# Strassen products for three index pairs of the convolution side in a one-core hybrid encoder layer

## The chip, the core and the metric

The kernel runs on 1 core of one Trainium2 chip (trn2). The time is that of one execution on the device, in microseconds (us); the median of several runs is given. One further execution was recorded by the hardware profiler, and every row below comes from it. Its span is the time from its first to its last instruction.

## The reference

One layer on 512 tokens behind 16 meta tokens (528 in all), model width 2048, float32:

```
hn = rmsnorm(h_res) * norm_in_g
P = hn @ w_in                     # 2048 x 8320
Pr, Pc = P[..., :RW_COLS], P[..., RW_COLS:]
...                               # RWKV-7 on Pr: token shift, decay, delta-rule state per head -> y_a
Bg, Cg, hc, g_c = four parts of Pc, 1024 columns each
y_b = Bg * causal_depthwise_conv(Cg * hc, conv_w, width 3) * silu(g_c)
h_res = h_res + concat([y_a, y_b]) @ w_out
out = rmsnorm(h_res)[:, 16:]
```

The recurrence runs over time: in chunks of 64 tokens it needs, for each pair of heads, decays, Gram matrices and an inverse, which are prepared ahead of it.

## The kernel before

Channels lie on partitions and time on the free axis. A float32 product is made of three float32r ones: the operand is cast to a high part, the rest is the low part, and high x high, high x low and low x high accumulate in one PSUM bank (`steps`, L314). The input x lives in SBUF split in this way (`xh`, `xl`, 16 slabs of 128 channels by 528 columns, scaled by the norm's gain).

The weights are 65 tiles of 128 output columns: r, k, v, g for eight pairs of heads, one low-rank tile, and B, C, h, gc for eight groups of the convolution side. A tile comes in two halves of 128 x 1024 (512 KB each). `prefetch` loads a half into one of three `raw` buffers through SP's DMA queue; `split_w` splits each of its two quarters: ScalarE (ACT) casts the high part (L124), VectorE (DVE) or GpSimd (POOL) subtracts for the low part (L125). There are six buffers each for high and low parts, so splits run at most three halves ahead of TensorE (PE). A tile is 96 matmuls of 256 to 264 columns, or 48 of 512 columns for B and gc. The order of tiles is the list `plan`; `stream` is the list of their halves (`halves` after the change).

PE's order is written out by hand. `mains` is a generator that yields after every matmul of a tile, and the preparation of the heads (`prepare`, `invert`) calls `fill(ns)` to run so much of it while other engines work; `until` runs it up to a given tile. `FW` holds these amounts. `later(ns, fn)` issues stores and loads after so much PE time. DVE, ACT, POOL and SP are ordered by a scheduler, and each then works in that fixed order: an instruction that waits holds up all behind it on its engine.

The stages in order: start (low rank, k0, r0, B0); preparation in four pairs of heads, with tiles as filler; recurrence over nine chunks (`recur`), with convolution tiles as filler; mixing; output projection, which already uses Strassen-Winograd products and sums of weights made by accumulating transfers (`add_by_transfer`, L1178: a DMA issued by POOL that adds to what lies at its destination). Before the change, the convolution tiles of indices 0 to 2 stand in the preparation, those of 3 to 7 in the recurrence and behind it.

The use of a tile is `use`: for the convolution side, C and h are scaled by the norm's factor and multiplied, the width-3 convolution is taken, then multiplied by B and by the gate of gc; the result goes to DRAM (`mixd`) until mixing.

Of the kernel before, what the change touches and what calls it, by code (L numbers as in the profile page):

```python
# [26 lines left out]
LP = NCH * CH  # L27
NPAIR = 8
ALPHA = -0.3032653298563167
RMS_EPS = 1e-6  # L30
# [46 lines left out]
def hymba_kernel(ctx: ExitStack, tc: tile.TileContext, xt, xtok, front, w_in, w_out, pv, lup, cst, msk, gf, out):  # L77
# [15 lines left out]
    gated = [dp.tile([P, SEQ], F32, tag=f"gated{j}", name=f"gated{j}", bufs=1) for j in range(NPAIR)]  # L93
    yd = dp.tile([2 * NPAIR * CH, SEQ], F32, tag="yd", name="yd", bufs=1)
    mixd = {j: dp.tile([P, SEQ], F32, tag=f"mixd{j}", name=f"mixd{j}", bufs=1) for j in range(NPAIR, KT)}

# [6 lines left out]

    stream = []
    plan = [("lora", 0), ("k", 0), ("r", 0), ("B", 0), ("v", 0), ("k", 1), ("r", 1), ("v", 1), ("g", 0), ("g", 1)]
    for j in range(0, NPAIR, 2):
        if j:
            plan += [(what, i) for i in (j, j + 1) for what in ("k", "r", "v")] + [("g", j), ("g", j + 1)]
        plan += [(what, j // 2) for what in ("C", "h", "B", "gc") if j or what != "B"]
    plan += [(what, i) for i in range(4, NPAIR) for what in ("C", "h", "B", "gc")]  # L110
    tile_of = {"r": 0, "k": 8, "v": 16, "g": 24, "lora": 32, "B": 33, "C": 41, "h": 49, "gc": 57}
    for what, i in plan:
        m = tile_of[what] + i
        stream += [w_in[m, :, 0:1024], w_in[m, :, 1024:2048]]
    stream[0:8] = [stream[j] for j in (0, 2, 4, 6, 1, 3, 5, 7)]
    N_IN = len(stream)
    stream += [w_out[0, g] for g in range(3)]
    quarters, chain, low = {}, {}, {}
    state = {"next": 0}

    def split_w(q, rq, eng):
# [4 lines left out]
        quarters[q] = (hi, lo)  # L126

    def prefetch(upto):
        while state["next"] < min(upto, len(stream) if chain else N_IN):
            j = state["next"]  # L130
            raw = chain[j - N_IN] if j >= N_IN else wp.tile([P, 1024], F32, tag="raw", name=f"wr{j}", bufs=3)
            state["dma"] = nc.sync.dma_start(raw, stream[j]).ins
            with tc.high_priority(offset=WEIGHTS):
                for q in range(2):
                    split_w(2 * j + q, raw[:, q * 512 : (q + 1) * 512], nc.gpsimd if q and 10 < j < N_IN else nc.vector)
            state["next"] = j + 1

    keep = ctx.enter_context(tc.tile_pool(name="keep", bufs=1, side="right"))
# [6 lines left out]
    rs = xp.tile([P, L], F32, name="rs")  # L145
    la = xp.tile([P, 2, L], F32R, name="la")
    ones = xp.tile([P, P + 2], F32R, name="ones")
    omm = xp.tile([P, 33], F32, name="omm")
    hv = xp.tile([P, 6, 8], F32, name="hv")
    hl = cp.tile([P, 2, 8], F32, name="hl")  # L150
    smask = xp.tile([P, NCH, CH], F32, name="smask")
    pm = ph1.enter_context(tc.tile_pool(name="pm", bufs=4, space=PSUM))
# [4 lines left out]

    tp = ph1.enter_context(tc.tile_pool(name="tp", bufs=1))

    def tr(name, dt=F32):  # L160
        return cq.tile([P, LP], dt, tag="tr", name=name, bufs=5)

    def tm(name):
        return tp.tile([P, LP], F32, tag="tm", name=name, bufs=3)


    warm = tp.tile([P, 1], F32, name="warm")
    nc.gpsimd.memset(warm, 0.0)
    cold = tp.tile([P, 512], F32, tag="tm", name="cold", bufs=3)
    nc.vector.memset(cold, 0.0)  # L170
# [34 lines left out]
    def load_w(n, tag):  # L205
        t = view(tag, 512)
        nc.sync.dma_start(t, stream[n][:, 512:1024])
        return t
# [112 lines left out]

    def main(j, ranges, name):
        prefetch(2 * j + 4)
        ps = banks(ranges, name, pm, "main")
        for k4 in range(4):
            if k4 == 1:
                prefetch(2 * j + 5)
            yield from steps(ps, ranges, k4, 4 * j + k4)
        return ps

    def scaled(ranges, ps, dst, base):
# [3 lines left out]
    def shift_full(ps, m, name, dst):  # L335
        pr = tp.tile([P, L + 1], F32, tag="pr", name=f"pr_{name}", bufs=2)
        nc.gpsimd.memset(pr[:, 0:1], 0.0)
        scaled(FULL, ps, pr, -1)
        sh = tm(f"sh_{name}")[:, 0:L]
        nc.scalar.activation(sh, pr[:, 0:L], AF.Copy, scale=col(V_MU, m))  # L340
        for (a, b), d in dst:
            nc.vector.scalar_tensor_tensor(
                out=d, in0=pr[:, a + 1 : b + 1], scalar=omm[:, m : m + 1], in1=sh[:, a:b], op0=ALU.mult, op1=ALU.add
            )

    def shift_real(ps, m, name, dst):
        pr = tp.tile([P, L + 1], F32, tag="pr", name=f"pr_{name}", bufs=2)
# [9 lines left out]

    def gate(g, name):
        th = tm(f"th_{name}")[:, 0:SEQ]
        nc.scalar.activation(th, g, AF.Tanh, scale=0.5)  # L360
        nc.vector.scalar_tensor_tensor(out=g, in0=th, scalar=1.0, in1=g, op0=ALU.add, op1=ALU.mult)
# [17 lines left out]
    def use(what, i, ps):  # L379
# [7 lines left out]
        elif what in ("r", "g"):  # L387
            t = cq.tile([P, SEQ], F32, tag=f"r{i % 2}" if what == "r" else "g", name=f"{what}{i}")
            shift_real(ps, tile_of[what] + i, f"{what}{i}", t)
# [8 lines left out]
        elif what == "h":  # L398
# [5 lines left out]
            nc.gpsimd.tensor_tensor(out=u[:, 0:n], in0=u[:, 0:n], in1=hh[:, 0:n], op=ALU.mult)  # L404
            cv = tp.tile([P, SEQ], F32, tag="cw", name=f"cv{i}")
            nc.scalar.activation(cv, u[:, 0:SEQ], AF.Copy, scale=col(V_CW, i))
# [5 lines left out]
            if i == 0:  # L412
                nc.gpsimd.tensor_tensor(out=cv, in0=cv, in1=got["B", 0], op=ALU.mult)
        elif what == "B":
            b = tm(f"b{i}")[:, 0:SEQ] if i else tp.tile([P, SEQ], F32, name="b0")
            with behind_of("split"):
                scaled(REAL, ps, b, META)
            got[what, i] = b
            if i:
# [15 lines left out]
    def token_scale_sums():  # L435
        pss = pi.tile([P, 8], F32, tag="misc", name="pss")
        for j, (a, b) in enumerate(((0, 128), (128, 256), (256, 384), (384, 512), (512, L))):
            nc.tensor.matmul(pss[0 : b - a, j : j + 1], accd[:, a:b], cs[:, C_ON : C_ON + 1], start=True, stop=True)
        var = tp.tile([P, 3, 8], F32, tag="nv", name="var0")
        nc.gpsimd.memset(var[:, 0], 1.0)  # L440
# [19 lines left out]
    def mains():  # L460
# [34 lines left out]
        use("B", 0, pd)  # L495
        for j in range(4, len(plan)):
            what, i = plan[j]
            rg = FULL if what in ("k", "v") else REAL if what in ("B", "gc") else TAIL
            ps = yield from main(j, rg, f"{what}{i}")
            if what == "B" and i < 4:  # L500
                state["split"] = low[4 * j + 4]
            use(what, i, ps)
# [36 lines left out]
    def until(*key):  # L539
        while key not in ready:  # L540
            step()
# [498 lines left out]
    for i in range(0, NPAIR, 2):  # L1040
        invert([prepare(i), prepare(i + 1)])
    until("g", NPAIR - 1)
    run_pending(float("inf"))
    ph2.close()
    with tc.tile_pool(name="ch", bufs=1, side="right", reuse_waits="tile") as ch:
        recur(ch)


# [69 lines left out]
    for _ in flow:  # L1118
        pass
    prefetch(len(stream))  # L1120
    ph1.close()
# [49 lines left out]
    def request(half, k, col, g):  # L1171
        t = wp.tile([P, 1024], F32, tag="raw", name=f"wo{half}{k}{col}{g}", bufs=3)
        state["dma"] = nc.sync.dma_start(t, rows_of(half, k, col, g)).ins
        straight[half, k, col, g] = t
# [321 lines left out]
```

## Time and profile before

| | |
|---|---|
| median of 3 runs | 1024.05 us (1023.93 to 1024.28) |
| span of the profiled execution | 1023.6 us (its own time is not listed apart; the span stands 0.45 under the median) |
| mean granted TensorE clock | 0.996 |
| PE busy | 1006.6 us, 9723 matmuls |
| DVE, ACT, POOL busy | 686.1, 393.8, 273.8 us |
| DMA | 174.82 MB, mean 171 GB/s |

A row of a profile names the line, engine, operation and tiles (output<-inputs). Busy time counts any time in which the engine had an instruction in flight; for PE, whose matmuls overlap, the duration in a row is longer than the distance from one matmul to the next. "Idle before <- X" names what ended an idle time. DMA share is the mean busy share of the 16 DMA engines.

### The profile page before, as it was taken

To read this page: it belongs to the slowest core of one execution; us is meant where nothing else is said; L and a number is where in the kernel's file an instruction comes from. 1 tells how busy PE (TensorE), PEld (TensorE's weight loads), DVE (VectorE), ACT (ScalarE), POOL (GpSimd) and SP (SyncE) were. 2 spreads that over 40 slices of the span, in tenths; PEclk is the share of its full clock that TensorE was granted. 3 is DMA by queue.
4 is the path that set the end of the run, shared out by engine and by line. 5 is a ranking of instruction groups with operands and counts; after the bars stand their busy time and mean duration, and the time that the engine had idled before them with its cause. 6 is when DMAs were issued, how large, how long until landed. Compare 5 with 4: busy or idle time off the path is not lost.

```text
span 1023.6 us, 23708 instructions
## 1 busy us (share of the span) xinstructions
PE 1006.6 (98%) x9723; PEld 919.0 (90%) x9723; DVE 686.1 (67%) x1239; ACT 393.8 (38%) x729; POOL 273.8 (27%) x292
## 2 busy tenths in 40 slices
PE   9999999999999999999999999999999999999996
PEld 8899998999988999998999998889889897787885
DVE  7677954587765569654669653244555697998787
ACT  7553423344313434322434322222222335445453
POOL 0122323233332323232322232123332332015001
PEclk9999999999999999999999999999999999999999
DMA  9526476546764364864263845867673688695754
GB/s 333 152 63 148 122 190 182 150 123 143 167 172 134 96 170 99 217 167 117 83 166 98 220 139 168 309 212 235 195 232 93 183 276 192 172 319 135 172 125 165
DMA packets 185036, 174.82 MB, mean 171 GB/s; under 512 B 121568, under 2 KB 142816, under 8 KB 184416
## 3 DMA queue, kind: packets, MB, share of 16 engines
q1 hardware_dynamic: 182336, 164.40, 55.8%
q0 software_dynamic: 2304, 8.39, 4.7%
q8 instruction: 76, 1.25, 0.5%
q10 hardware_dynamic: 288, 0.52, 0.1%
q14 instruction: 32, 0.26, 0.1%
HBM read 136.92 MB, written 36.35 MB: 169 GB/s over the span
## 4 chain that ended last, share of the span: by engine, by line
PE 68%; DVE 8%; DMA 4%; issue 2%; SPq 1%; ACT 1%; POOL 0%; DVEq 0%; ACTq 0%; POOLq 0%
PE ps_gc L314 8%; PE ps_h L314 8%; PE ps_B L314 7%; PE ps_k L314 7%; PE ps_v L314 7%; PE ps_C L314 7%; PE ps_g L314 7%; PE ps_r L314 7%; DVE ol L1193 3%; DMA wo<-in_w_out_dram 2%; PE M L1220 2%; PE g L659 1%; PE zs L984 1%; PE Q L1220 1%; DVE xb L1201 1%
## 5 line engine op out<-in xcount | busy, mean ns | idle before, releaser
L125 POOL TENSOR_TENSOR wl<-wr,wh 128x512 fp32r<-128x512 f32 x119 | 169.2, 1423 | 370.8 <-ACT wh L124 356.4
L124 ACT CAST wh<-wr 128x512 fp32r<-128x512 f32 x252 | 152.7, 618 | 294.8 <-PE ps_C L314 51.9
L125 DVE TENSOR_TENSOR wl<-wr,wh 128x512 fp32r<-128x512 f32 x133 | 100.9, 765 | 109.0 <-ACT wh L124 108.6
L314 PE MATMUL ps_k<-xh,wl 128*128 128x264 f32 x256 | 73.1, 286 | 1.1 <-DVE wl L125 1.1
L314 PE MATMUL ps_v<-xh,wh 128*128 128x264 f32 x256 | 73.0, 285 | 0.0
L314 PE MATMUL ps_h<-xh,wh 128*128 128x258 f32 (+1 forms) x256 | 72.8, 284 | 0.0
L314 PE MATMUL ps_k<-xh,wh 128*128 128x264 f32 x256 | 72.8, 284 | 0.0
L314 PE MATMUL ps_v<-xl,wh 128*128 128x264 f32 x256 | 72.7, 284 | 0.0
L314 PE MATMUL ps_v<-xh,wl 128*128 128x264 f32 x256 | 72.7, 284 | 0.0
L314 PE MATMUL ps_k<-xl,wh 128*128 128x264 f32 x256 | 72.6, 284 | 0.0
L314 PE MATMUL ps_C<-xh,wh 128*128 128x258 f32 (+1 forms) x256 | 72.6, 284 | 0.0
L314 PE MATMUL ps_h<-xh,wl 128*128 128x258 f32 (+1 forms) x256 | 72.3, 282 | 0.2 <-issue 0.2
L314 PE MATMUL ps_r<-xh,wh 128*128 128x258 f32 (+1 forms) x256 | 72.4, 283 | 0.0
L314 PE MATMUL ps_g<-xl,wh 128*128 128x258 f32 (+1 forms) x256 | 72.3, 282 | 0.0
L314 PE MATMUL ps_r<-xl,wh 128*128 128x258 f32 (+1 forms) x256 | 72.2, 282 | 0.0
L314 PE MATMUL ps_g<-xh,wl 128*128 128x258 f32 (+1 forms) x256 | 72.0, 281 | 0.0
L314 PE MATMUL ps_C<-xl,wh 128*128 128x258 f32 (+1 forms) x256 | 72.0, 281 | 0.0
L314 PE MATMUL ps_g<-xh,wh 128*128 128x258 f32 (+1 forms) x256 | 72.0, 281 | 0.0
L314 PE MATMUL ps_h<-xl,wh 128*128 128x258 f32 (+1 forms) x256 | 71.9, 281 | 0.0
L314 PE MATMUL ps_r<-xh,wl 128*128 128x258 f32 (+1 forms) x256 | 71.9, 281 | 0.0
L314 PE MATMUL ps_C<-xh,wl 128*128 128x258 f32 (+1 forms) x256 | 71.9, 281 | 0.0
L314 PE MATMUL ps_B<-xh,wl 128*128 128x512 f32 x128 | 51.3, 401 | 0.0
(353 smaller groups left out, 3006.2 us busy)
## 6 DMA issues: line engine op xcount, KB each, us to landing
wr<-in_w_in_dram SPq DMA_DIRECT2D x126, 512.0 KB
ct<-opd SPq DMA_DIRECT2D x64, 288.0 KB
wo<-in_w_out_dram SPq DMA_DIRECT2D x24, 512.0 KB
x<-in_w_out_dram POOLq DMA_DIRECT2D x16, 512.0 KB, 6.2
opd<-ar SPq DMA_DIRECT2D x8, 576.0 KB
opd<-gt SPq DMA_DIRECT2D x16, 288.0 KB
opd<-bt SPq DMA_DIRECT2D x64, 64.0 KB
x<-in_w_out_dram SPq DMA_DIRECT2D x8, 512.0 KB
```

The costliest lines, as they stand in the source:

```text
L124: nc.scalar.copy(hi, rq)
L125: low[q] = eng.tensor_tensor(out=lo, in0=rq, in1=hi.bitcast(F32), op=ALU.subtract).ins
L314: nc.tensor.matmul(ps[r], ww[:, w], xx[:, kt, a:b], start=(kt == 0 and n == 0), stop=(kt == KT - 1 and n == 2))
L659: nc.tensor.matmul(z[h][:, c - c0], bk[hs, c, h : h + 2, :].rearrange("p a s -> p (a s)"), ar[hs, c].rearrange("p a s -> p (a s)"), start= ...
L984: nc.tensor.matmul(d[hs, j], w, x[hs], start=(a == 0), stop=(a == b - 1))
L1193: nc.vector.tensor_tensor(out=lo, in0=rq, in1=hi.bitcast(F32), op=ALU.subtract)
L1201: nc.vector.tensor_tensor(out=h, in0=h, in1=ps, op=op)
L1220: nc.tensor.matmul(bank[s], left(prod, jj, m, s), w, start=(jj == 0 and n == 0), stop=(jj == 7 and n == 2))
```

## The change

For indices 1, 2 and 3 of the convolution side the pairs (C, h) and (B, gc) are computed by Strassen's seven products. The 2 x 2 blocks are: two halves of the 2048 input channels, two tiles of output columns, two halves of the time (columns from 14 and from 270). A product is 24 matmuls of 258 (C, h) or 256 (B, gc) columns, with K = 1024; there are 3 x 2 x 7 = 42. The name M5(2,1) means product M5 for index 2, pair (B, gc); the list SPREAD writes it 521.

- Sums of weights: M1, M2, M3 use a plain half. M5 and M7 load one half into a raw buffer, then POOL issues a transfer that adds another. M6 does so with two further halves, in a tile of its own (`Y`); M4 adds a fourth to what M6 used.
- Forms of x: the four quarters of x are scaled by the gain and stored to DRAM (`scaled_rows`); forms F6, F5, S3, F3 are loaded and added by transfers (`form`) and split into `fh`, `fl`, which hold one form at a time.
- Sums of products: M1, M2, M6, M4 are combined on ACT and DVE and stored to DRAM (`partd`); M5, M7, M3 are copied out of PSUM and added in DRAM by POOL's transfers (`take`).
- In the recurrence, `finish_couple` (Z1 to Z3) loads the results, and does what `use` did.
- The order: all 42 products stand in the preparation, among k, r, v, g; index 0's C, h, gc move to its end; g6 and g7 too. `solve` and `solve_first` in FW grow by 6000 ns. The three raw buffers get names of their own; several tiles move between pools; B0's result waits in DRAM.

The core of the diff:

```diff
+HW = 258
...
-    evac=34, start=1062, lora=2200, gram=8000, gram_b=13500, gram2=5500, misc=2000, v=2000, vt=1000, solve=24500, solve_first=30000,
+    evac=34, start=1062, lora=2200, gram=8000, gram_b=13500, gram2=5500, misc=2000, v=2000, vt=1000, solve=30500, solve_first=36000,
...
+SPREAD = (
+    "v0 X11 k1 X00 r1 X01 v1 F6 g0 g1 g2 g3 110 k2 210 610 r2 v2 410 111 k3 211 "
+    "611 r3 v3 X10 411 120 220 620 k4 r4 420 121 221 621 k5 v4 421 130 230 630 r5 v5 "
+    "430 131 231 631 k6 r6 431 F5 k7 v6 510 511 520 521 530 531 S3 r7 v7 710 711 720 "
+    "721 730 731 F3 g4 g5 310 311 320 321 330 331 g6 g7 C0 h0 gc0 C4 h4 Z1 B4 gc4 "
+    "C5 Z2 h5 B5 gc5 C6 Z3 h6 B6 gc6 C7 h7 B7 gc7"
+)
...
+        if item[0] == "M6":
+            jobs.append((max(free_at[-2], f - 14, form_of["F6",] + 2), f, "sum", item))
...
+        elif item[0] in ("M5", "M7"):
+            jobs.append((f - 6, f, "sum", item))
...
+    def start(job):
...
+        if prod == "M6":
+            t = fp.tile([P, 4 * HW], F32, tag="Y", name=f"y{i}{s}", bufs=2)[:, 0:1024]
+            parts_ = [(0, 0), (1, 0), (1, 1)]
+        else:
+            t = take_slot(f"x{prod}{i}{s}")
+            parts_ = [(1, 0), (0, 0) if prod == "M5" else (1, 1)]
+        state["dma"] = nc.sync.dma_start(t, half_of(i, s, *parts_[0])).ins
+        for p in parts_[1:]:
+            nc.gpsimd.dma_start(t, half_of(i, s, *p), accum_op=ALU.add)
...
+    def follow(item, t):
+        if item[0] == "M6":
+            nc.gpsimd.dma_start(t, half_of(item[1], item[2], 0, 1), accum_op=ALU.add)
...
+    def form(name):
+        first, *others = FORMS[name]
+        for c in range(2):
...
+            nc.sync.dma_start(t, quarters_d[first][:, ks])
+            for x in others:
+                nc.gpsimd.dma_start(t, quarters_d[x][:, ks], accum_op=ALU.add)
+            nc.scalar.copy(fh[:, ks], t)
+            nc.vector.tensor_tensor(out=fl[:, ks], in0=t, in1=fh[:, ks].bitcast(F32), op=ALU.subtract)
...
+    def take(item):
...
+        nc.scalar.copy(t, bank)
+        if prod == "M3":
+            nc.gpsimd.dma_start(d[:, 2], t, accum_op=ALU.add)
+        else:
+            nc.gpsimd.dma_start(
+                d[:, 2:4] if prod == "M5" else d[:, 1:4:2], t.unsqueeze(1).to_broadcast([P, 2, n]), accum_op=ALU.add
+            )
```

More of the change, by code (lines that the diff above doesn't have):

```diff
@@ L128, in prefetch, with summed @@
+    def summed(item):
+        prod, i, s = item
+        t = running.pop(item)
+        return t, None if prod in ("M6", "M4") else t
+    def follow(item, t):
+        if item[0] == "M6":
+            nc.gpsimd.dma_start(t, half_of(item[1], item[2], 0, 1), accum_op=ALU.add)
+            running["M4", item[1], item[2]] = t
     def prefetch(upto):
-        while state["next"] < min(upto, len(stream) if chain else N_IN):
+        end = len(halves) if chain else N_IN
+        while state["next"] < min(upto, end):
@@ L130, in prefetch @@
             j = state["next"]
-            raw = chain[j - N_IN] if j >= N_IN else wp.tile([P, 1024], F32, tag="raw", name=f"wr{j}", bufs=3)
-            state["dma"] = nc.sync.dma_start(raw, stream[j]).ins
+            for job in [job for job in jobs if job[1] <= j]:
+                start(job)
+            slot = None
+            if isinstance(halves[j], tuple):
+                raw, slot = summed(halves[j])
+            else:
+                if j >= 8 and j < N_IN:
+                    raw = slot = started.pop(j)
+                else:
+                    raw = chain.get(j - N_IN) if j >= N_IN else None
+                    if raw is None:
+                        raw = slot = take_slot(f"wr{j}")
+                    state["dma"] = nc.sync.dma_start(raw, halves[j]).ins
@@ L135, in prefetch @@
                     split_w(2 * j + q, raw[:, q * 512 : (q + 1) * 512], nc.gpsimd if q and 10 < j < N_IN else nc.vector)
+            if isinstance(halves[j], tuple):
+                follow(halves[j], raw)
+            if slot is not None:
+                free.append((slot_of.pop(id(slot)), j + 1))
             state["next"] = j + 1
+        seen = False
+        for job in list(jobs):
+            if job[0] > state["next"] or job[1] > state["next"] + 16:
+                break
+            chained_ = job[3][0] == "M6" if job[2] == "sum" else False
+            if chained_:
+                start(job)
+            elif not seen and any(at_ < state["next"] for n, at_ in free):
+                start(job)
+            else:
+                seen = True
     keep = ctx.enter_context(tc.tile_pool(name="keep", bufs=1, side="right"))
```

278 lines of the change are left out of this document (236 added, 42 removed).

## The prediction

> **What bounds the kernel now.** I read the page first: spans, the 40 slices, the chain that ended last, the costliest groups.
>
> ```profile
> span 1023.6 us, 23708 instructions
> PE 1006.6 (98%) x9723; PEld 919.0 (90%) x9723; DVE 686.1 (67%) x1239; ACT 393.8 (38%) x729; POOL 273.8 (27%) x292
> DMA  9526476546764364864263845867673688695754
> PE 68%; DVE 8%; DMA 4%; issue 2%; SPq 1%; ACT 1%; POOL 0%; DVEq 0%; ACTq 0%; POOLq 0%
> L125 POOL TENSOR_TENSOR wl<-wr,wh 128x512 fp32r<-128x512 f32 x119 | 169.2, 1423 | 370.8 <-ACT wh L124 356.4
> L124 ACT CAST wh<-wr 128x512 fp32r<-128x512 f32 x252 | 152.7, 618 | 294.8 <-PE ps_C L314 51.9
> L125 DVE TENSOR_TENSOR wl<-wr,wh 128x512 fp32r<-128x512 f32 x133 | 100.9, 765 | 109.0 <-ACT wh L124 108.6
> ```
>
> PE is busy 98% and carries 68% of the chain, so a matmul that goes is time that goes, as long as PE is fed. POOL is busy 27% and waits 356 us for casts that themselves wait for PE: the splitters run just in time, not late. The DMA digits are mostly between 3 and 7 up to slice 24, the preparation, so there is room there, but not twice over. The profiled execution has a span of 1023.6; the median of the runs is 1024.05, so I add 0.45 for what lies around the span. A measurement of this kernel can tell about 0.2% (2 us) from no change.
>
> **Matmuls: -15.4.** Next the windows of the last four conv tiles (C, h, B, gc of index 7), where nothing else runs on PE. Columns: stretch, its length, busy time (and starts) of each engine, clock, DMA share, GB/s.
>
> ```profile
> 810.13:821.54 11.41, 11.41 (x98) 11.41 (x98) 10.94 (x17) 4.72 (x9) 2.57 (x2) 1.00 0.70 205
> 821.54:832.95 11.41, 11.41 (x97) 11.41 (x97) 11.41 (x15) 3.10 (x6) 4.64 (x2) 1.00 0.93 264
> 832.95:844.06 11.11, 11.11 (x49) 9.01 (x49) 10.94 (x18) 5.20 (x11) 3.78 (x3) 1.00 0.82 273
> 844.06:855.20 11.14, 11.14 (x50) 9.03 (x49) 5.42 (x7) 2.50 (x5) 5.26 (x4) 1.00 0.84 219
> ```
>
> C or h is 96 matmuls of 256 or 258 columns in 11.41: 0.119 each. B and gc are 48 of 512 columns in 11.11 and 11.14. A Strassen product is 24 matmuls of 256 or 258 columns: 24 x 0.119 = 2.85. Indices 1 to 3 lose 3 x (11.41 + 11.41 + 11.11 + 11.14) = 135.2 and get 42 x 2.85 = 119.8.
>
> **A stall of the old order: -3.8.** The timeline of PE in index 1's B tile, and the clock behind it:
>
> ```profile
> 306.45 1.14 PE L831 MATMUL t<-xn,gt 64*64 64x64 f32 x32 [2.24 <-DVE xn L822]
> 306.40:308.40 2.00, 1.95 (x34) 1.74 (x35) 0.00 (x0) 0.78 (x2) 0.00 (x0) 0.50 0.85 254
> 308.40:310.40 2.00, 2.00 (x7) 1.55 (x7) 0.69 (x1) 1.33 (x3) 0.54 (x1) 0.66 0.86 306
> ```
>
> PE waits 2.24 for the first solve's transposes, then runs at clock 0.50 and 0.66 for two windows of 2 us: 1.0 + 0.7 more, 3.9 in all, of which I take 3.8. The change puts 6 us more filler ahead of each solve, and this order of tiles is gone. Its bounds are 0 (the wait returns elsewhere) and 3.8. From these rows I charge 1.6 us of clock to every wait of 2 us or more below. The Trainium skill (TensorE: Matmul & The Clock Gate, What's actually happening) lets the array fall to half clock only after an idle window of about 3.4 us. By that rule a wait of 2 to 3 us would cost no clock; here 2.24 us did, so the measurement decides.
>
> **What an accumulating transfer costs.** The before kernel has 16 of them, in the output projection. I look for one alone on the queues, then a stretch with four (POOL issues) and two plain loads, then plain loads alone, then two stretches of the preparation.
>
> ```profile
> L1178 POOL DMA_DIRECT2D x<-in_w_out_dram x16: 867/884/1169, 847.4 to 990.3; - x16
> DMA to landing us min/median/max: 5.5/6.2/9.5
> 936.48 0.90 POOL L1178 DMA_DIRECT2D x<-in_w_out_dram  x1 [3.12 <-DVE ol L1193]
> 939.83 0.89 POOL L1178 DMA_DIRECT2D x<-in_w_out_dram  x1 [0.96 <-DVE ol L1193]
> 943.18 0.89 POOL L1178 DMA_DIRECT2D x<-in_w_out_dram  x1 [0.96 <-DVE ol L1193]
> 945.08 1.17 POOL L1178 DMA_DIRECT2D x<-in_w_out_dram  x1
> 938.00:942.00 4.00, 3.81 (x17) 2.78 (x16) 3.81 (x5) 2.41 (x7) 2.83 (x3) 1.00 0.80 143
> 938.00:955.00 17.00, 16.53 (x70) 12.73 (x69) 15.06 (x19) 10.57 (x20) 6.12 (x6) 1.00 0.90 186
> 906.00:907.00 1.00, 1.00 (x6) 0.81 (x5) 1.00 (x3) 0.10 (x1) 0.00 (x0) 1.00 1.05 410
> 430.00:480.00 50.00, 50.00 (x552) 44.59 (x551) 29.04 (x67) 14.56 (x26) 14.51 (x13) 1.00 0.57 159
> 480.00:580.00 100.00, 100.00 (x858) 98.51 (x857) 66.48 (x122) 38.70 (x72) 28.82 (x32) 1.00 0.51 132
> ```
>
> One 512 KB accumulation holds all 16 DMA engines for 4.00 x 0.80 = 3.2 us. A plain one takes 0.524 MB / 410 GB/s x 1.05 = 1.34. They add: 4 x 3.2 + 2 x 1.34 = 15.5, and the 17 us at 0.90 are 15.3 (186 GB/s x 17 = 3.16 MB, six halves). So an accumulation costs 2.4 loads, needs POOL for 0.88 and lands 6.2 after its issue.
>
> The change adds 62 of them: 30 weight terms, 14 for the forms of x, 18 that add products into DRAM. Most sums M6 and M4 are started up to 14 halves ahead in tiles of their own, so their latency is hidden. M5 and M7 are not: six each in a row, through the three raw slots.
>
> The stretch from the first M5 load (when k7 starts) to the last M7 has, on PE, three tiles k7, v6, v7 of about 11.65, r7 of 11.4, eleven products of 2.85, and about 10 of small matmuls: 88.
>
> ```profile
> 479.68 11.65 PE ps_k L314 x96
> 299.39 3.96 DMA wr<-in_w_in_dram
> ```
>
> DMA in it: 12 weight terms and 9 form terms (last of F5, S3, F3) accumulated, 21 x 3.2 = 67; ten results into DRAM, half a transfer each, 10 x 1.6 = 16 (not in the trace; 264 KB at either rate is 0.7 to 1.6, short rows may cost more); 16 weight loads and 5 first terms, 21 x 1.34 = 28; the preparation's own traffic, from the last two windows (79.5 of 150 us, less 26 loads, 45 for a pair of heads), 22 for one. Sum 133, against 88: PE could lose 45 there.
>
> The Trainium skill (DMA: Bandwidth & Descriptors, Measured (HBM→SBUF, 128 partitions, SWDGE, issued from GpSimd)) gives 341 GB/s for 1 MB issued from GpSimd. An estimate from that page is 1.5 us for 512 KB, 36 us less over the 21, which leaves only the waits of the next part and a sum of 1024.5. The row of 3.2 us decides against it.
>
> **Waits that the order fixes: the lower bound.** In the built program, POOL's order around M5 is (each line waits in turn):
>
> ```
> accumulate M5(2,0); M5(1,0) result into DRAM; split M5(2,0)
> M5(1,1) result into DRAM; M5(2,0) result into DRAM
> accumulate M5(2,1); accumulate M5(3,0); split M5(2,1); ...
> ```
>
> The second weight term of M5(2,1), PE's very next product, is issued only after M5(2,0) has left PE.
>
> ```profile
> L940 ACT ACTIVATE pn<-rz x18: 378/383/387, 643.6 to 780.5; 128x256 f32<-128x256 f32 x18
> ```
>
> PE waits 0.38 (copy out) + 0.9 (issue of the result) + 6.2 (landing) + 0.62 (cast) + 0.5 (the first low part's 0.77 less two matmuls) = 8.6, and 1.6 of clock: 10. Queued behind it on POOL are the split of M5(2,1) and the term of M5(3,1). In M7, the term of M7(3,1) stands behind the split of M7(3,0): from M7(3,0)'s landing PE needs 1.4 + 2.85 + 1.1 (gram matmuls), the other term 1.24 + 1.42 + 6.2 + 0.62 = 9.5, so 4 and 1.6 of clock: 6. Together 16 even if nothing else is on the queues. Between 16 and 45 I take the middle, **+31**: transfers add, as 938 to 955 shows, but some of the 133 (results, stores of operands) may come late without harm.
>
> **Start of the recurrence: +3.7.**
>
> ```profile
> 627.25 0.42 SPq L913 DMA_DIRECT2D ct<-opd  x1
> 634.09 10.22 SPq L913 DMA_DIRECT2D ct<-opd  x15
> L932 PE MATMUL rz<-ct x288: 218/218/267, 642.8 to 779.9; 64*64 64x64 f32 x144
> ```
>
> Before, the first chunk's loads leave at 627 and from 634 on, 8 us or more ahead of their use at 642.8. Now SP holds the eighth behind a weight load that needs the split of B4's first half, whose buffers C4's second half frees: 2 x 0.62 + 1.42 + 0.75 issues + 3.96 landing = 7.4 after C4 ends, and the recurrence wants it 3.7 after (22 matmuls of h4 at 0.119, then 14 small ones of its own). Bounds 0 and, with clock, 5.3.
>
> **At nothing.** 36 more casts (22 us of ACT), 18 more POOL splits (26 us) and 62 issues (55 us): POOL goes to about 355 of 1024 busy, in what it now waits for casts; without that cover each late split would cost up to 1.42. The forms' casts and the couples' conv steps replace like work. Output stage unchanged.
>
> **Sum.** 1023.6 - 15.4 - 3.8 + 31 + 3.7 = 1039.1, with 0.45: **1039.5**.
>
> **Rivals.** *Hidden (0.22).* Stores and forms slip into gaps and only the two POOL waits remain, at the shortest landing 5.5, the recurrence on time: 16 - 1.4 = 14.6, 1024.05 - 19.2 + 14.6 = 1019.5, or 1017 if M7's wait goes too. For it: the digits leave room before and after. It wins over no change as soon as the stretch and the recurrence lose under 19. *Order alone (0.14).* No queueing, 6.2 landings, recurrence late: 1024.05 - 19.2 + 16 + 3.7 = 1024.5. *Deeper (0.18).* Result rows of 1 KB cost twice (16 more), and the stretch loses all it can: 1024.05 - 19.2 + 45 + 3.7 + 6 = 1060 with part of the 16 hidden. *Not what it says* (256-column matmuls slower in these orders): the C and h windows have such matmuls, so no chance of its own. The forecast keeps 0.46.
>
> **Numbers.** Range 1018 to 1060: the hidden case's price below, the deeper one's above, a tenth left out at each end; the likeliest case alone is 1030 to 1048. Faster by over 0.2%: the hidden case and a little of order alone, 0.24. Within: half of order alone, 0.07. Slower: 0.69.
>
> **What would show it.** PE busy near 991; idle of PE in front of M5(2,1) of 8 or more and of M7(3,1) of 4 or more, ended by splits that wait for DMA; DMA digits 8 to 9 in slices 16 to 21, software queue near 18% of the span; landing of accumulations there above 6.2; clock dips after each. Wrong: PE idle in that stretch under 15 us, or landings at 5.5 with DMA digits of 6.

## The result and the profile after

The changed kernel takes 1150.38 us (median of 4 runs, 1147.57 to 1154.22) against 1023.99 for the kernel before in the same series (1023.54 to 1024.28): a ratio of 1.1235, interval 1.1208 to 1.1262, or 126.4 us more. The forecast was 1039.5, its range 1018 to 1060. The profiled execution took 1152.68 with a span of 1150.9.

The page of the changed kernel, the lines that answer to those shown of before:

```profile
span 1150.9 us, 24483 instructions
PE 1040.8 (90%) x9867; PEld 958.5 (83%) x9867; DVE 721.2 (63%) x1274; ACT 436.7 (38%) x829; POOL 366.6 (32%) x375
PEclk9999899899988999987789898979999999999999
DMA  9437889675797767887998797487668569686754
L167 ACT CAST wh<-wr 128x512 fp32r<-128x512 f32 x240 | 143.3, 617 | 196.8 <-DMA wr<-in_w_in_dram 40.9
q0 software_dynamic: 12768, 35.47, 17.6%
```

What ends most of ACT's idle time in front of these casts, cause by cause, has changed from a tile of PE's (51.9 us) to a landing (40.9 us of 196.8; the waits for PE's tiles together are still more). So the splitters, which ran just in time, are late in places. The DMA digits are up nearly everywhere in the preparation, not only in the stretch of M5 and M7. PE is busy for longer than before although it does less, because the clock is lower (PEclk).

Where the time went, by stage. The first matmul of the recurrence starts at 642.8 before and at 756.8 or 756.9 after, the last chunk's at 779.9 and 906.7. Windows of before, then of after (columns as in the prediction):

```profile
0.00:642.80 642.80, 636.31 (x5871) 604.99 (x5871) 425.57 (x848) 244.54 (x454) 177.67 (x209) 1.00 0.57 154
642.80:779.90 137.10, 136.51 (x2612) 121.23 (x2615) 62.98 (x108) 35.92 (x69) 42.01 (x36) 1.00 0.70 220
```

```profile
0.00:756.90 756.90, 666.17 (x6027) 641.52 (x6028) 457.61 (x876) 286.15 (x551) 269.11 (x290) 0.93 0.77 194
756.90:906.70 149.80, 141.32 (x2615) 124.69 (x2615) 65.25 (x114) 38.11 (x73) 43.66 (x38) 0.95 0.71 221
```

The preparation is 114 longer, the recurrence 12.7, the rest is the same. In the preparation PE is idle 90.7 in place of 6.5, which is 84; the matmuls should save 15.4; so the lower clock (0.93) takes about 45 (an estimate: what is left of the 114). The waits of PE, grouped by what they waited for (us in total, times, longest):

```profile
PE M L475 <- ACT wh L167: 35.3, 7, 11.1
PE t L1111 <- DVE xn L1102: 11.4, 3, 6.3
PE g L939 <- DVE bk L918: 11.0, 3, 5.4
PE M L475 <- POOL wl L168: 5.9, 3, 2.7
PE z L1166 <- ACT tm L1159: 5.0, 1, 5.0
```

Some 41 us are products that wait for their weights (L475). Some 27 in these rows are steps of the heads (t, g, z): the filler is long enough only if DVE, ACT and POOL keep up, and here they stand in front of late landings. The waits that the prediction named are there, in the timeline (start, duration, engine; the idle time before in brackets):

```profile
515.04 1.21 POOL L557 DMA_DIRECT2D part<-M  x1 [4.26 <-issue]
515.77 1.43 POOL L196 DMA_DIRECT2D xM<-in_w_in_dram  x1
...
524.00 1.14 ACT L167 CAST wh<-xM 128x512 fp32r<-128x512 f32 x2 [9.98 <-DMA xM<-in_w_in_dram]
...
524.67 0.58 PE L475 MATMUL M<-fh,wh 128*128 128x256 f32 x1 [11.06 <-ACT wh L167]
...
616.40 0.58 PE L475 MATMUL M<-fh,wh 128*128 128x256 f32 x1 [4.70 <-ACT wh L167]
```

POOL issues the result of M5(2,0), then the second term of M5(2,1), which lands 8 us later; PE waits 11.06 (8.6 were forecast). In front of M7(3,1) it waits 4.70 (4 forecast). But the timeline also shows a wait that was not in the prediction, some 270 us earlier, behind a sum of M6:

```profile
236.31 0.88 POOL L196 DMA_DIRECT2D y<-in_w_in_dram  x1 [3.90 <-DMA y<-in_w_in_dram]
...
238.18 1.99 POOL L897 TENSOR_SCALAR tz<-tz 128x576 f32<-128x576 f32 x1
240.20 2.44 DVE L899 TENSOR_TENSOR_SCAN cc<-smask,tz 128x576 f32<-128x576 f32 x1 [6.35 <-POOL tz L897]
...
251.19 3.56 PE L939 MATMUL g<-ar,bk 64*128 64x128 f32 x32 [3.85 <-DVE bk L918]
```

POOL stands in front of each term until the one before has landed; a step of the heads (tz) is queued behind; DVE waits for it; and PE, at the end of that chain, waits for the Gram operands.

### The profile page after: what moved, and what is told of

The parts are those of the page before. It is cut to its first block, busy times and chain, and to the rows that moved or that the text cites. A ratio compares the mean times of both kernels' runs of the same rounds, so it can differ in the third digit from the quotient of the medians.

```text
span 1150.9 us, 24483 instructions
## 1 busy us (share of the span) xinstructions
PE 1040.8 (90%) x9867; PEld 958.5 (83%) x9867; DVE 721.2 (63%) x1274; ACT 436.7 (38%) x829; POOL 366.6 (32%) x375
## 5 line engine op out<-in xcount | busy, mean ns | idle before, releaser
L167 ACT CAST wh<-wr 128x512 fp32r<-128x512 f32 x240 | 143.3, 617 | 196.8 <-DMA wr<-in_w_in_dram 40.9
L168 DVE TENSOR_TENSOR wl<-wr,wh 128x512 fp32r<-128x512 f32 x127 | 104.0, 824 | 86.1 <-ACT wh L167 85.8
L475 PE MATMUL M<-fh,wh 128*128 128x258 f32 (+1 forms) x192 | 61.5, 321 | 35.4 <-ACT wh L167 35.3
L438 PE MATMUL ps_r<-xh,wl 128*128 128x258 f32 (+1 forms) x256 | 75.3, 294 | 0.0
L475 PEld LDWEIGHTS M<-fh,wh 128*128 128x128 f32 x192 | 42.5, 221 | 37.4 <-ACT wh L167 32.6
L475 PE MATMUL M<-fh,wl 128*128 128x258 f32 (+1 forms) x192 | 61.4, 320 | 6.0 <-POOL wl L168 3.3
L475 PE MATMUL M<-fl,wh 128*128 128x258 f32 (+1 forms) x192 | 59.9, 312 | 0.0
L438 PEld LDWEIGHTS ps_k<-xh,wl 128*128 128x128 f32 x256 | 49.3, 192 | 5.7 <-DVE wl L168 5.2
L438 PEld LDWEIGHTS ps_r<-xh,wl 128*128 128x128 f32 x256 | 51.5, 201 | 0.5
L438 PEld LDWEIGHTS ps_r<-xh,wh 128*128 128x128 f32 x256 | 51.4, 201 | 0.4
```

The lines of the kernel that those rows point to most:

```text
L167: nc.scalar.copy(hi, rq)
L168: low[q] = eng.tensor_tensor(out=lo, in0=rq, in1=hi.bitcast(F32), op=ALU.subtract).ins
L438: nc.tensor.matmul(ps[r], ww[:, w], xx[:, kt, a:b], start=(kt == 0 and n == 0), stop=(kt == KT - 1 and n == 2))
L475: nc.tensor.matmul(bank, ww[:, w], x[:, kt], start=(kt == 0 and n == 0), stop=(kt == 7 and n == 2))
```

## The experiments

"More" is against the kernel before, run in the same series. The changed kernel stands at 126.4 more.

**What the transfers cost: e1 to e4.** Leave accumulating transfers out.

```diff
-            nc.gpsimd.dma_start(t, half_of(i, s, *p), accum_op=ALU.add)      # start, follow  (e1; e2: M6, M4; e3: M5, M7)
-                nc.gpsimd.dma_start(t, quarters_d[x][:, ks], accum_op=ALU.add)  # form  (e1, e4)
-            nc.gpsimd.dma_start(d[:, 2], t, accum_op=ALU.add)  # and the other of take  (e1, e3)
```

> All 62 added accumulating transfers are left out: each sum of weights is its first half, each form of x its first quarter, and the results of M5, M7 and M3 are not added in DRAM. Matmuls, casts, splits and plain loads stay. Theory A (POOL waits in its queue for one accumulation before it can issue the next, and all behind it is late) and theory B (the 16 DMA engines are full, so every landing is late) both expect nearly all of the loss back: 1024 - 15.4 (matmuls) - 3.8 (old stall) + 13 (the late start of the recurrence, which stays) = 1018, say 1010 to 1028, PE idle in the preparation under 15 us. Theory C (the products themselves, their casts or the order of the tiles cost the time) expects over 1070.

> Only the 18 accumulations for M6 and M4 are left out (these sums are their first half). In the changed kernel the stretch from 150 to 450 us has 29 us of idle PE and some 17 lost to a lower clock. A expects nearly all of it back, since in that stretch POOL stands 47 us in front of accumulations of these sums: 1150 - 40 = 1110. B expects back what 18 x 3.2 = 58 us less on the DMA engines bring in 310 us where their share is 0.78: it would be 0.6, so also most, about 1115. If the waits there are those of the heads' preparation alone, under 10 us come back. This run prices the stretch.

> Only the 12 accumulations into the weights of M5 and M7 and the 18 of results in DRAM are left out. In the changed kernel 480 to 680 us has 45 us of idle PE and some 25 lost to a lower clock. My prediction had this stretch as the whole cost, 16 to 45. A and B expect 1150 - 60 = 1090, with 5 to 10 of idle left in front of the forms. Were the stretch bound by the forms of x or the heads' steps, under 25 us come back.

> Only the 14 accumulations for the forms of x are left out (each form is its first quarter). A expects 15 us back: POOL seldom waits for them (6.5 us), but ACT stands 16 us in front of the last ones, with a wait of PE of 5.0 behind it at 558. B expects more, 14 x 3.2 = 45 us of engine time out of full stretches, so 30 or more. No effect beyond 5 us would put them off the path.

| | time | more | ratio, interval | back |
|---|---|---|---|---|
| e1, all 62 out | 1059.58 | 34.6 | 1.0347 (1.0304 to 1.0390) | 91.8 |
| e2, M6 and M4 | 1128.29 | 103.3 | 1.0997 (1.0961 to 1.1034) | 23.1 |
| e3, M5, M7, results | 1110.47 | 85.5 | 1.0846 (1.0824 to 1.0868) | 40.9 |
| e4, forms | 1126.56 | 101.6 | 1.0999 (1.0970 to 1.1028) | 24.8 |

The three groups add up to 88.8 of 91.8. So the accumulations are 92 of the 126, spread over three groups, 1.3 us each for M6 and M4, 1.4 for M5, M7 and the results, 1.8 for the forms. The prediction had priced the second group and part of the third. e2 and e3 gave back less than either theory expected, and e4 lies between the two, so these runs price the groups but do not choose between A and B. With none of the transfers 34.6 stay where 1018 was expected, outside every interval named for e1: something else costs too.

**Engine time or POOL's order: e5 to e8.** The same transfers without adding; the M6 chain apart in POOL's order; results without POOL; more filler ahead of the recurrence.

```diff
-            nc.gpsimd.dma_start(t, half_of(i, s, *p), accum_op=ALU.add)
+            nc.gpsimd.dma_start(t, half_of(i, s, *p))          # e5; also in follow and form
...
+                with tc.issue_after(low[2 * j + 1]):            # e6: the two terms of M6, two halves apart
+                    nc.gpsimd.dma_start(running[item], half_of(item[1], item[2], *todo.pop(0)[1]), accum_op=ALU.add)
...
+        later(3500, lambda: nc.sync.dma_start(d[:, k], t))      # e7: partd has 7 blocks; added after fetch, on DVE
...
-    ... begin=19500 ...
+    ... begin=25500 ...                                         # e8
```

> The 44 accumulations of weights and forms stay in place, in the same order and chains on POOL and with the same bytes read, but they overwrite instead of adding, so the sums are their last term (results are still added in DRAM). Theory A (the chain: POOL waits for each landing before the next issue) expects that most of the cost stays, since count, order and chain are the same and only the landing is shorter: 1115 to 1135. Theory B (engine time: an adding transfer holds the 16 engines 3.2 us, a plain one 1.34) expects the 44 x 1.86 = 82 us of engine time to come back for the most part: 1080 to 1095. That such transfers cost the same when they add or not would leave 1150.

> The same transfers with the same bytes, but the sums of M6 start as soon as their tile is free (10 halves ahead of use and not 3), and their two accumulations are issued two halves apart, each behind the split of a half on POOL, so POOL does not stand in front of a landing; the last quarter of x is stored later, behind F5. A expects back what leaving these transfers out gave, 22, and no wait of PE behind a sum of M6: about 1128. B expects nothing, the engine time is the same: 1145 to 1155.

> The results of M5, M7 and M3 are stored plainly by SP and added on DVE when the recurrence loads them (four additions for each pair, one more load), in place of 18 accumulations in DRAM by POOL. My prediction had the wait of 10 in front of M5(2,1) hang on the result of M5(2,0) on POOL; A expects that wait and half of the 40 us that the third run gave: 1130. B expects 18 x 1 us of engine time in full stretches: 1140. If the weight terms alone are the cost there, under 5 comes back.

> 6 us more filler of PE stand ahead of the recurrence (begin 25500 in place of 19500), nothing else. In the changed kernel the first chunk's loads leave SP behind three weight loads, and PE loses 12.9 us from 757 to 768 against before, 9.0 of it idle and the rest clock. If this is the order on SP, 6 us of work fill 6 of the idle time and the clock stays up: 8 to 11 back, 1140. If the loads are late because the engines are full (DMA share 1.0 there), the wait moves with the start: under 3 back.

| | time | more | ratio, interval |
|---|---|---|---|
| e5, 44 without adding | 1113.57 | 88.0 | 1.0857 (1.0833 to 1.0880) |
| e6, M6 chain apart | 1159.34 | 133.8 | 1.1294 (1.1263 to 1.1326) |
| e7, results plain | 1143.63 | 118.1 | 1.1153 (1.1115 to 1.1190) |
| e8, filler | 1149.57 | 124.0 | 1.1198 (1.1170 to 1.1227) |

e5 comes out at the edge of A's interval, far from B's. But B's interval rests on 1.34 us for a plain transfer, and those that POOL issues held the engines 1.7 (worked out in the last section): 52 us of engine time went and not 82, and 38 us came back. So e5 does not decide between A and B. And e6, which was to show A, gave nothing back, it is 7 slower. POOL's waits in front of the M6 terms are nearly gone in it; the row of the waits in after, and that in e6:

```profile
POOL y L196 <- DMA y<-in_w_in_dram: 38.3, 7, 7.9
```

```profile
POOL y L208 <- DMA y<-in_w_in_dram: 7.7, 4, 3.7
```

and PE waits in other places. From 150 to 200, after and e6:

```profile
150.00:200.00 50.00, 42.46 (x360) 41.35 (x359) 28.98 (x59) 14.71 (x26) 16.34 (x18) 0.96 0.86 200
```

```profile
150.00:200.00 50.00, 33.97 (x253) 32.83 (x253) 22.37 (x48) 10.58 (x18) 11.74 (x14) 0.87 0.91 217
```

```profile
184.33 0.59 PE L454 MATMUL ps_k<-xh,wh 128*128 128x264 f32 x1 [6.07 <-ACT wh L167]
```

The sums that start earlier meet the first forms, the DMA share rises to 0.91, and now plain weights (here of a k tile) come late. So A falls as the whole cause: a wait on POOL that goes is paid elsewhere. In e7 the wait in front of M5(2,1) fell from 11.06 to 3.52, as A and the prediction had it, but the kernel gained 8 where A expected 20; its timeline:

```profile
519.11 0.48 PE L475 MATMUL M<-fh,wh 128*128 128x256 f32 x1 [3.52 <-ACT wh L167]
```

e8 gave 2.4 for its 6 us of filler, which its interval does not tell from nothing. In its trace the recurrence starts 4.1 later and its last chunk stands where it did, at 906.7.

**What is left, and load by itself: e9 to e12.**

```diff
# e9: e1 and, in form(), no transfer at all
+            nc.scalar.copy(fh[:, ks], xh[:, k : k + 4, a : a + HW].bitcast(F32))
+            nc.vector.tensor_copy(fl[:, ks], xl[:, k : k + 4, a : a + HW].bitcast(F32))
# e10: kernel before, in prefetch
+            if 14 <= j < 98 and j % 2 == 0:
+                with tc.issue_after(low[2 * j + 1]):
+                    nc.gpsimd.dma_start(extra, w_in[j % 64, :, 0:1024], accum_op=ALU.add)
# e11: kernel before
-    ... solve=24500, solve_first=30000,
+    ... solve=30500, solve_first=36000,
# e12: SPREAD from F5 on
+    "F5 k7 510 511 v6 520 521 r7 530 531 S3 v7 710 711 g4 720 721 g5 730 731 F3 310 ..."
```

> The first run (no accumulation at all, 1059.6) with the 24 plain transfers of x left out too: no quarter is loaded, stored or read back, and each form is a copy of one quarter of the split x in SBUF (same casts and copies on ACT and DVE). Theory B (the loss follows the time that added transfers hold the DMA engines, where a stretch has little room) expects that the 24 x 1.34 = 32 us of engine time, all of it in the stretches in front of the forms, come back at about the rate of the other runs (0.45 to 0.85 us for each us): 1059 - 15 to - 27 = 1032 to 1044. If what is left in that run is the order of the tiles and the filler of the heads' steps, under 5 comes back.

> The kernel before with 42 accumulating transfers of 512 KB added, one for every tile of the preparation, issued by POOL behind the split of a half, into a tile that nobody reads. Nobody waits for them, and they stand 11 us apart, so POOL does not wait either. They are 42 x 3.2 = 134 us of engine time, as many as the sums of weights and forms in the change. B in its plain form (each us of engine time costs 0.45 to 0.85) expects 1084 or more. B of stretches (only where the share comes near 1) expects less, since the share goes evenly from 0.57 to 0.78: 1035 to 1060. If consumers that wait for their own sum are what costs, and not the load: under 1030.

> The kernel before with solve = 30500 and solve_first = 36000 alone. My prediction took 3.8 off for the wait of 2.24 in front of the first solve's transposes and the clock behind it: 1020.2. If the wait only moves to another place: 1024.

> The changed kernel with another order of tiles from F5 on: M5 and M7 stand two at a time between k7, v6, r7, v7, g4 and g5, in place of six in a row; the transfers are the same. B of stretches expects that PE's work around them takes up part of the 43 us that leaving them out gave: 15 to 25 back, 1125 to 1135. If the sums are bound by the three raw buffers, which the ordinary tiles now share, nothing comes back.

| | time | more | ratio, interval |
|---|---|---|---|
| e9, no transfers of x either | 1038.79 | 14.0 | 1.0135 (1.0121 to 1.0149) |
| e10, 42 added that nobody waits for | 1043.19 | 18.4 | 1.0178 (1.0157 to 1.0200) |
| e11, solve alone | 1028.39 | 3.6 | 1.0037 (1.0024 to 1.0049) |
| e12, other order | 1171.26 | 146.5 | 1.1456 (1.1420 to 1.1493) |

The 24 plain transfers of x, with the 32 scalings on ACT that go with them (14.3 us of ACT, which the edit takes out too), cost 20.6 (34.6 less 14.0). e9's windows, then e10's preparation:

```profile
0.00:643.20 643.20, 627.46 (x6025) 609.05 (x6026) 447.01 (x876) 276.10 (x519) 225.65 (x228) 0.99 0.60 167
643.20:793.10 149.90, 141.49 (x2615) 125.08 (x2615) 65.34 (x114) 38.10 (x73) 43.73 (x38) 0.95 0.71 222
```

```profile
0.00:662.40 662.40, 641.33 (x5869) 608.73 (x5870) 426.81 (x848) 243.81 (x454) 210.80 (x252) 0.98 0.76 183
```

e9's preparation is as long as before's (643.2 and 642.8) although it has 15.4 us less of matmuls: idle PE (15.7 against 6.5) and the clock take the whole gain, with no accumulation and no transfer of x (the DMA share is 0.60, against 0.57 before). e10 brings the DMA share of the preparation from 0.57 to 0.76, as much as the change does, and costs 18, as B of stretches had it: load alone, evenly spread, is a fifth of the 92. Its trace shows where: PE's waits for the heads' inverse (t<-xn) are 16.1 us in place of 2.2. The longest ends a round trip through DRAM, two small plain transfers of the heads' own (sx<-y, then xT<-sx, here with the time from issue to landing), the first of which took under 3 us before:

```profile
PE t L836 <- DVE xn L827: 16.1, 4, 9.1
```

```profile
298.15 7.88 DMA sx<-y
...
308.57 5.90 DMA xT<-sx
```

e11 is slower: 50 more matmuls stand ahead of the recurrence, which starts 8.2 later, and what follows is only 3.6 shorter. e12, where sums share the raw buffers with ordinary tiles, is 20 slower than the change, which none of its cases expected; products there also wait 17.8 us for forms of x.

**Why transfers that something waits for cost more: e13 to e18.**

```diff
# e13: M5 and M7 of index 1 in the Y tiles
+        if prod == "M6" or i == 1:
# e15: kernel before; the 42 accumulations go onto the raw halves
+            if 14 <= j < 98 and j % 2 == 0:
+                nc.gpsimd.dma_start(raw, w_in[j % 64, :, 0:1024], accum_op=ALU.add)
# e16: e10 with
-            if 14 <= j < 98 and j % 2 == 0:
+            if 14 <= j < 98 and j % 1 == 0:
# e17: e15 and e18: kernel before, each with
+                cq.tile([P, 1024], F32, tag="raw3", name=f"wr{j}") if 14 <= j < 98 and j % 4 == 1
```

> The changed kernel with the sums of M5 and M7 for index 1 in the two tiles of the M6 sums, free by then, so that four of twelve sums start as soon as their form is split, some 20 us ahead of use, and the three raw buffers serve the other eight. Transfers and engine time are the same. Theory L (a sum holds a buffer from its load to its split, about 12 us, and three buffers give one product each 4 us where PE needs 2.85) expects the waits of 6.3 and 11.1 in the row of M5 to fall under 8 in all and those of M7 under 5: 1125 to 1135. Theory B (engine time) expects 1145 to 1155.

> The kernel before with the same 42 accumulations as e10_load, but each added onto a half of an ordinary tile between its load and its split (the weights are then wrong sums), so PE waits for each. L expects little more than e10_load's 1043, since a half of an ordinary tile takes PE 5.7 us and three raw buffers are 17 us, more than a load and a landing (4 + 8): 1045 to 1060. If every awaited transfer costs by itself, the rate of the change, 92 x 42 / 62 = 62: 1085 or more.

> The kernel before with 84 accumulations that nobody waits for, one for each half of the preparation, 5.7 us apart: 268 us of engine time, which takes the share from 0.57 to 0.98. If the cost were in proportion it would be twice e10_load's 18: 1061. B of stretches expects that near a full share every load and round trip of the heads' steps comes late, and the cost grows faster: 1090 to 1130.

> e15_await with four raw buffers in place of three, so each load and its accumulation start one half, 5.7 us, earlier; transfers, casts and order of use are the same. Theory H (ACT works in a fixed order and stands in front of a cast whose sum has not landed, while steps of the heads that PE needs next stand behind it) expects ACT's waits for landings to fall from 151 to under 60 and the time to come down to about that of the transfers that nobody waits for: 1040 to 1055. Were it the engine time of the transfers in the place where they are issued, it stays: 1075 to 1085.

> The kernel before with four raw buffers in the preparation, nothing added. Its loads come in time already, so H expects no change, 1022 to 1026.

| | time | more | ratio, interval |
|---|---|---|---|
| e13, own buffers | 1152.99 | 127.7 | 1.1238 (1.1219 to 1.1256) |
| e15, e10's transfers, awaited | 1081.13 | 55.8 | 1.0556 (1.0524 to 1.0588) |
| e16, e10's twice | 1115.03 | 89.7 | 1.0878 (1.0847 to 1.0908) |
| e17, e15 with four buffers | 1086.14 | 60.8 | 1.0588 (1.0549 to 1.0626) |
| e18, before with four buffers | 1024.44 | -0.9 | 0.9990 (0.9981 to 1.0000) |

L falls: own buffers for four sums change nothing that the interval shows, and PE's waits in the row of M5 fall from 20.3 to 18.2 only, where L expected under 8. e15 is the telling one: transfers that cost 18 when nobody waits cost 56 when each is part of a half that is used, 1.33 each, near the 92 / 62 = 1.48 of the change. PE itself waits little for those weights (some 14 us). ACT's waits for weights, before and then in e10, e15 and e17 in turn (us, times, longest; in e15 POOL, too, stands in front of loads before it can issue the term):

```profile
ACT wh L124 <- DMA wr<-in_w_in_dram: 13.5, 5, 4.7
```

```profile
ACT wh L124 <- DMA wr<-in_w_in_dram: 60.5, 12, 7.5
```

```profile
ACT wh L124 <- DMA wr<-in_w_in_dram: 150.9, 30, 10.2
POOL wr L134 <- DMA wr<-in_w_in_dram: 45.0, 12, 6.9
```

```profile
ACT wh L124 <- DMA wr<-in_w_in_dram: 145.9, 24, 12.2
```

and in the changed kernel:

```profile
ACT wh L167 <- DMA xM<-in_w_in_dram: 53.5, 9, 10.0
ACT wh L167 <- DMA wr<-in_w_in_dram: 40.9, 13, 6.7
ACT wh L167 <- DMA y<-in_w_in_dram: 21.2, 3, 10.6
```

The casts stand in ACT's fixed order among the steps of the heads, and the low parts in DVE's, so while one engine stands in front of a landing the steps behind it wait too. The time of e10 and e15 goes with ACT's waits. A place in e15 shows the path: ACT's cast waits until 193.81 for its sum to land, DVE stands 9.67 us in front of the low part, and the heads' xn, whose operand's load was issued at 175, stands behind it; PE then waits 4.79 for xn:

```profile
194.46 0.69 DVE L125 TENSOR_TENSOR wl<-wr,wh 128x512 fp32r<-128x512 f32 x1 [9.67 <-ACT wh L124]
195.07 0.71 DVE L824 STREAM_TRANSPOSE xn<-xT 128x512 f32<-128x512 f32 x1
```

PE's waits for xn are 24.1 us in e15. Of the four, this one and the longest (9.29) stand directly behind such a low part, the other two (5.54 and 4.45) behind round trips as in e10. For the changed kernel, whose longest waits are for its own sums, the split was not shown. e17, which was to shorten ACT's waits, did not (145.9), so H was not put to the test: POOL issues the term in its order behind the same splits. At the place above the term leaves at 184.45 in place of 186.12, and the cast starts at 193.84 in place of 193.81. e16's 90 can't be read as evenly spread load alone either, for there POOL stood 248 us in front of its own added transfers; PE's waits for xn are 36.3 in it, each behind a late load of xT.

**What can be bought back: e19.** All products and the weight sums stay.

```diff
# form(): quarters from xt, scaled and added on DVE; no quarters_d; results as in e7; begin=25500
+                            nc.vector.scalar_tensor_tensor(
+                                out=t[:, h + m], in0=u[:, m], scalar=g, in1=t[:, h + m], op0=ALU.mult,
+                                op1=ALU.subtract if x[3:] else ALU.add,
+                            )
```

> The changed kernel with the forms of x made from plain loads (quarters of x are loaded again, scaled and added on DVE with one operation for each block of 128 channels; 14 accumulations, 8 stores and 8 loads of quarters go, 8 loads come, some 24 us of DVE are added), results stored plainly and added when the recurrence loads them, and 6 us more filler ahead of the recurrence; the 30 accumulations of weights stay. If the prices of the single runs add up (24 for the accumulations of forms, 7 of the 21 for plain transfers of x, 8 for the results, 2 for the filler): 1150 - 41 = 1109. If the additions on DVE take their place in the heads' chain: 1130 or more. It stays above the kernel before either way.

1128.70, 103.8 more, ratio 1.1008 (1.0965 to 1.1051): 22.6 back of the 41 that the prices add up to, near the case in which the additions on DVE take their place in the heads' chain (1130 or more). Its longest group of PE's waits shows where the rest went:

```profile
PE M L475 <- ACT fh L520: 27.9, 3, 11.6
```

The products now wait for the forms (11.6 at the longest), which are built one term after another. No version of the changed kernel came below the kernel before.

## Why the prediction was wrong

The mechanism it named is there, the sign and the wait it placed are right; it priced one stretch of a cost that runs through the whole preparation, and took the waits of the others as nothing. Its steps in order:

- *Matmuls, -15.4.* Right in size. Twenty-two gaps between starts in M5(3,0) at full clock:

```profile
531.79 0.28 PE L475 MATMUL M<-fh,wh 128*128 128x258 f32 x1
...
534.44 0.28 PE L475 MATMUL M<-fl,wh 128*128 128x258 f32 x1
```

  are 2.65, or 0.120 each. But busy time was expected near 991 and is 1040.8, since a matmul at half clock counts twice.
- *Old stall, -3.8.* Wrong. The same wait (t<-xn) is there three times, 11.4 in all, and e11 shows that the larger solve amounts by themselves cost 3.6 (the wait becomes three there, 2.5 in all). With no accumulation and no transfer of x (e9) 14.0 are left, of which 12.8 are the recurrence: so -15.4 is met by +16.6 of waits and clock of the new order. A stall that goes was booked without asking what comes late next.
- *M6 and M4 hidden: 0.* The step that failed first. "Started up to 14 halves ahead" was read from the list of jobs; the list is worked off in the order of use, and each sum starts 3 halves ahead of its split, with a load and two landings in a row. In front of three of the six ACT then stands, 18 to 24 us after the load was issued. Measured 23 (e2). That the short lead alone makes the 23 was not shown: e6 started the sums some 10 halves ahead and gained nothing.
- *Forms.* Nine of their fourteen accumulations and five of the 24 plain transfers of x were in the 133, the rest in no sum. Measured 25 (e4) and 21 (e9, with ACT's scalings).
- *M5, M7, results: +31.* Measured 41 (e3), between its bounds of 16 and 45. The two are not quite the same sum: the stretch had nine form terms and ten of the results in it, e3 takes out all 18 results and no form term. The price of a transfer was near. From the rows of the software queue of before, after and e7 (packets, MB, share of the span):

```profile
q0 software_dynamic: 2304, 8.39, 4.7%
```

```profile
q0 software_dynamic: 8640, 31.52, 15.4%
```

  the 62 took 0.176 x 1150.9 - 0.047 x 1023.6 = 154 us; e7, without the 18 results, has 0.154 x 1138.7 = 175, so these took 27, 1.5 each (1.6 forecast), and the other 44 took 2.9 each (3.2). The estimate of 1.5 for 512 KB, worked out from the Trainium skill (DMA: Bandwidth & Descriptors, Measured (HBM→SBUF, 128 partitions, SWDGE, issued from GpSimd)), does not hold for these: the trace has 2.9. The plain ones of e5, 1.7 each, come near it.
- *Start of the recurrence, +3.7, at most 5.3.* Measured 12.7. The mechanism is the one named, but two weight loads and not one stand between the first chunk's loads on SP. e9 has the same order there and a recurrence as long, 149.9, without any accumulation; so the accumulations are not what makes them late. (The DMA engines are full with these loads, before as after: a share of 1.04 from 642 to 647 and of 1.03 from 762 to 768.)

```profile
751.54 1.33 SPq L1193 DMA_DIRECT2D ct<-opd  x3
755.17 0.33 SPq L185 DMA_DIRECT2D wr<-in_w_in_dram  x1
...
756.07 1.87 SPq L1193 DMA_DIRECT2D ct<-opd  x4
759.89 0.33 SPq L185 DMA_DIRECT2D wr<-in_w_in_dram  x1
760.32 7.55 SPq L1193 DMA_DIRECT2D ct<-opd  x9
```

- *At nothing: casts, POOL's splits and issues.* POOL is at 367 as forecast (355), but its cover was only looked at as busy time. Both POOL and ACT lose their slack in waiting: 116 us of ACT in front of weights alone (13.5 before).
- *Clock, 1.6 for each wait of 2 us or more.* Right for a short one (the last section shows it), and charged twice; the preparation has sixteen such waits, most of them longer, and its lower clock takes 45.

The rivals stopped at 1060 for the same reason: each was a variant of the one stretch. None held that the cost per transfer would be as high in the stretches called hidden, which is what e2 and e4 showed. What stays open is how the 1.5 us for each accumulation of the change splits between the engines' fixed orders (ACT, DVE, POOL) and full stretches of the DMA. The traces of e10 and e15 show both ways at work; e6, e13 and e17 were each to take one candidate away and moved the waits without shortening the kernel.

## What to carry to other kernels

A transfer that is planned ahead can be hidden only if its issue, in the engine's real order, comes a landing ahead of use: look for that distance in the built order, not in the list that planned it. It is not enough by itself, as e6 showed. Where engines work in a fixed order, price an added transfer by the queues that will stand in front of its landing (here ACT's casts, DVE's low parts and POOL's next term, with the heads' steps behind), not by the share of busy time. And test a "freed" DMA share by adding the traffic that nobody waits for, and then the same traffic awaited: here 18 and 56 us.

## What the runs showed of the hardware

After a wait of 2.91 us the half clock came only when PE was at work again, 2.1 us after the wait. Timeline row and windows:

```profile
539.04 0.39 PE L475 MATMUL M<-fh,wh 128*128 128x256 f32 x1 [2.91 <-ACT wh L167]
```

```profile
541.00:541.40 0.40, 0.40 (x4) 0.40 (x4) 0.40 (x2) 0.40 (x2) 0.18 (x1) 0.64 0.87 215
...
542.00:543.00 1.00, 1.00 (x7) 1.00 (x6) 1.00 (x4) 0.00 (x0) 1.00 (x2) 0.50 0.66 221
```

The clock is 0.50 from 541.1 (0.64 is the mean of 0.11 us at full and 0.29 at half clock) to 544.5 (0.98 in the half microsecond behind it), 3.4 us, which cost 1.7; the prediction charged 1.6. The Trainium skill (TensorE: Matmul & The Clock Gate, What's actually happening) has the array fall to half clock after an idle window of about 3.4 us and come back after a busy one as long. The length of the slow stretch agrees; the idle time does not, 2.91 us were enough.

A plain transfer of 512 KB that POOL issues holds the engines less than an accumulating one, but is no cheap stand-in. The software queue of e5:

```profile
q0 software_dynamic: 12768, 35.47, 13.6%
```

That is 0.136 x 1107.9 = 151 us; less the 48 of the output projection and 27 of the results, 44 plain ones took 75, or 1.7 each in place of 2.9. The engine time fell by 52 us and 38 came back.
